# Moving a small subtraction to GpSimd, issuing weight loads earlier and re-timing two divisions in a two-layer hybrid encoder

## The chip, the cores and the metric

The kernel runs on one core of one Trainium2 chip. The metric is the device time of one execution, in microseconds. The core has five engines that run side by side and wait for each other by semaphores: TensorE (PE in the profile), VectorE (DVE), ScalarE (ACT), GpSimd (POOL), and SyncE (SP), which here issues nearly all DMAs. Each engine takes its own instructions in the order of the program, so an instruction that waits holds up everything behind it on its engine. The same is true of the DMA issues on SP.

## The reference

The reference is a trunk of two layers over 512 grid tokens and 16 learned "meta" tokens, with a model width of 1024. Cut to what matters here:

```python
def hybrid_layer(x, ...):
    h = rms_norm(x, norm_g)
    proj = einsum('bld,de->ble', h, w_in)            # 5376 columns
    qa, ka, va, za, qb, kb, vb, zb, ga, gb = split_cols(proj)
    qa, ka = rope(rms_norm(qa)), rope(rms_norm(ka))  # 8 query heads, 2 key/value heads
    oa = gqa_attention(qa, ka, va) * silu(za)        # every query sees all 528 keys
    ob = neighbourhood_attention(qb, kb, vb, rpb) * silu(zb)
    ya, yb = oa @ w_o_attn, ob @ w_o_na
    mixed = sigmoid(ga) * ya + sigmoid(gb) * yb
    return x + mixed @ w_out
```

The last step is a final RMS norm over the 512 grid tokens. The "global branch" is `gqa_attention`; the "meta keys" are the 16 meta tokens among its 528 keys.

## The kernel before

**Precision by parts.** Every float32 operand of a large product is split in two: a high part, which is a cast to the format `fp32r`, and a low part, which is the difference. A product is then three matmuls: high by high (L325), low by high (L326), high by low (L327). For a weight, ScalarE casts the high part (`whi`, L240) and GpSimd subtracts for the low part (`wlo`, L241).

**Weights in halves.** A weight chunk of 128 output columns comes as two halves of 128x512 numbers, 256 KB each. `order` is the list of all 210 halves in the sequence of their use. `weights()` (L231) is called for half `n`: it issues the loads (`raw`, L235) up to a certain place in the list and the casts and subtractions up to place `n + 2`. There are four buffers each for `raw`, `whi` and `wlo`, so a load must wait until the subtraction four halves earlier has read its buffer, and a cast until TensorE is done with the half four places earlier.

**A planner by half tiles.** TensorE works through the projections (function `product`), and after each half tile (12 or 24 matmuls with weights from memory) `tick()` lets two side plans take a step. One side plan, `side_gqa`, carries the global branch, the other, `side_na`, the neighbourhood branch. Each unit of a side plan (two 128-query tiles of one head of the global branch, or one head of the neighbourhood branch) is a list of steps, and the tables `GQA_AT` and `NA_AT` (L37 to L40) give the half tile after the unit's start at which each step is written. A list scheduler then orders each engine's instructions by priority and readiness; parts marked as high priority go first. When the projections run out, `side_na.finish()` and `side_gqa.finish()` write all remaining steps at once.

**One unit of the global branch.** `scores` computes the products of queries and keys and the exponentials. `turn` transposes 32x32 blocks on VectorE (L867) and writes the result to DRAM (`turn`, L870). `back` (L872) reads it again, transposed in full, by four DMAs (L877), and the 16+16 meta columns by a fifth into the tile `pm` (L880). `split_part` (L885) makes the high and low parts `pth` and `ptl` of the probabilities with `split` (L193 on ScalarE, L194 on VectorE). `split_ends` (L891) does the same for the meta keys: two casts on ScalarE (L896) and two subtractions on VectorE (L898) into a single padded tile `ga`, 32 partitions by 128 elements each, since a unit has two query tiles. `sums` (L901) then accumulates nine matmuls (L905): eight on `pth` and `ptl`, the ninth and last on `ga`. The two units of meta queries have one cast and one subtraction of 32x64 each.

**Inverse sums.** The softmax is not divided at once. `divided_later` (L801) has three steps for a pair of heads: `turned` takes the reciprocals of the row sums, transposes them and writes them to DRAM by four small DMAs (L811); `spread` reads them back on 64 partitions each by two DMAs (L817); `multiplied` multiplies the branch's SiLU gate by them on GpSimd (L822: `za` for the global branch, `zb` for the neighbourhood branch). The gate then multiplies the branch's output on VectorE (L777). The table entry `"divide"` gives the half tiles of the three steps.

Of the kernel before, what the change touches and what calls it, by code (L numbers as in the profile page):

```python
# [11 lines left out]
F32 = mybir.dt.float32  # L12
# [21 lines left out]
DEPTH = 2  # L34


GQA_AT = ({"scores": (0, 1), "turn": (1, 2), "back": 3, "split": (5, 5), "ends": 5, "divide": (3, 4, 6), "sums": (7, 7)},  # L37
          {"scores": (0, 1), "turn": (1, 2), "back": 3, "split": (5, 5), "ends": 5, "divide": (3, 4, 6), "sums": (7, 7)})
NA_AT = ({"stages": (0, 2, 5, 5, 5, 7), "values": (3, 4), "divide": (3, 4, 6)},
         {"stages": (0, 2, 4, 5, 5, 7), "values": (3, 4), "divide": (3, 4, 6)})  # L40

NORM_AT = ({"tokens": (0, 1, 3), "squares": (1, 1, 2, 3, 2), "heads": (2, 3, 5, 7, 6), "values": (1, 4)},
           {"tokens": (1, 3, 5), "squares": (2, 2, 2, 3, 2), "heads": (2, 3, 5, 7, 6), "values": (1, 4)})
# [52 lines left out]
def trunk_kernel(ctx: ExitStack, tc: tile.TileContext, xT, w, gn, gf, bias, rope, out):  # L96
    nc = tc.nc
# [15 lines left out]
    def slot(tag, name, dt=F32):  # L113
        n = NKEY if tag in ("KB", "KR", "K", "E") else NTOK
        t = slots.tile([P, n], dt, tag=tag, bufs=BUFS[tag], name=name)
        return t[:, :NTOK] if tag == "E" else t
# [8 lines left out]
    def bank(pool, name, tag):  # L125
        return pool.tile([P, 512], F32, tag=tag, name=name)
# [44 lines left out]
    def pad_tile(kind):  # L171
        padded[kind].rotate(1)
        return padded[kind][0]
# [17 lines left out]
    def split(hi, lo, src):  # L191
        with tc.high_priority():
            split_at["hi"] = nc.scalar.copy(hi, src)  # L193
            split_at["any"] = nc.vector.tensor_sub(lo, src, hi.bitcast(F32))  # L194
# [12 lines left out]
    order = []  # L207
    for l in range(DEPTH):
# [4 lines left out]
        if l == 0:  # L213

            order = order[6:]
# [6 lines left out]
    ready, loaded = [], []  # L222
# [7 lines left out]

    def weights(l, c, half, ahead=3):  # L231
        n = place[l, c, half] + ahead
        for l_, c_, i in order[len(loaded):n + 1]:
            raw = slots.tile([P, 4 * P], F32, tag="raw", bufs=BUFS["raw"], name=f"raw{l_}_{c_}_{i}")
            nc.sync.dma_start(raw, w[l_, c_][:, 4 * P * i:4 * P * (i + 1)])  # L235
            loaded.append(raw)
        for l_, c_, i in order[len(ready):n]:
            name, raw = f"{l_}_{c_}_{i}", loaded[len(ready)]
            hi, lo = (slots.tile([P, 4 * P], F32R, tag=tag, bufs=BUFS[tag], name=tag + name) for tag in ("whi", "wlo"))
            cast = nc.scalar.copy(hi, raw)  # L240
            sub = nc.gpsimd.tensor_sub(lo, raw, hi.bitcast(F32))  # L241
            split_at["weights"] = cast.ins, sub.ins
            ready.append((hi, lo))
        return ready[place[l, c, half]]
# [175 lines left out]
    def next_weights():  # L420
        weights(0, QA + 3, 0, 1)
        done[:] = split_at["weights"]
# [11 lines left out]
    first, ends = {}, ((0, HALF), (HALF, NTOK))  # L434
# [19 lines left out]
    for l in range(DEPTH):  # L454
# [136 lines left out]
        qs, turn = [], None  # L591
        for j in range(4):
# [188 lines left out]
        def rows2(v):  # L781
            return v.rearrange("p s d -> p (s d)")
# [64 lines left out]
        def global_unit(kv, parts, n, name, done):  # L847

            width = n * len(parts)
            per = min(4, 512 // width)  # L850

            first_token = (0, NMETA)
            c = {"t": []}

            def scores(i):
                q, qs, scale, total = parts[i]
                if i == 0:
                    c["both"] = slots.tile([P, 2 * NTOK], F32, tag="M", bufs=BUFS["M"], name=f"P{name}")
                    c["p"] = [c["both"][:, NTOK * t:NTOK * (t + 1)] for t in range(len(parts))]
                softmax(c["p"][i], q, qs, kv, NMETA - first_token[i], n, scale, total, f"{name}_{i}")  # L860

            def turn(i):

                a, b = (0, NREAL) if i == 0 and len(parts) > 1 else (NREAL * i, NREAL * i + NREAL + 32)
                if len(parts) == 1:
                    nc.gpsimd.memset(c["both"][:n, NTOK:b], 0.0)
                nc.vector.transpose(c["both"][:n, a:b], c["both"][:n, a:b])  # L867
                if i == len(parts) - 1:
                    c["there"] = dpool.tile([P, 2 * (NREAL + 32)], F32, tag="turned", bufs=3, name=f"turn{name}")
                    nc.sync.dma_start(c["there"][:n, :b], c["both"][:n, :b])  # L870

            def back():  # L872

                w, there = width * 4, c["there"][:n].rearrange("(b j) (t f) -> j t b f", j=32, t=2)
                for q in range(4):
                    r = slice(32 * q, 32 * q + 32)
                    nc.sync.dma_start(c["both"][r, :w].rearrange("j (t b x) -> j t b x", t=len(parts), x=P),  # L877
                                      there[:, :len(parts), :, P * q:P * q + P])
                c["meta"] = tiny.tile([32, P], F32, tag="meta", name=f"pm{name}")
                nc.sync.dma_start(c["meta"][:, :n].rearrange("j (b i) -> j b i", i=32),  # L880
                                  c["there"][:n].rearrange("(b j) f -> j b f", j=32)[:, :, NREAL:NREAL + 32])

            def split_part(kt):
                v = c["both"][:, :width * 4].rearrange("p (x k i) -> p x k i", k=4, i=32)[:, :, kt:kt + per]
                th, tl = slot("G", f"pth{name}_{kt}", F32R), slot("G", f"ptl{name}_{kt}", F32R)  # L885
                split(*(t[:, :width * per].rearrange("p (k x i) -> p x k i", k=per, i=32) for t in (th, tl)), v)
                for i in range(per):
                    for v in (th, tl):
                        c["t"].append((VA2[:, kt + i, kv], v[:, width * i:width * (i + 1)]))

            def split_ends():  # L891

                tm, m = pad_tile("ga"), c["meta"][:, :n]
                with tc.high_priority():
                    for t in range(len(parts)):
                        nc.scalar.copy(tm[32 * t:32 * t + 32, n * t:n * (t + 1)], m)  # L896
                    for t in range(len(parts)):
                        nc.vector.tensor_sub(tm[64 + 32 * t:96 + 32 * t, n * t:n * (t + 1)], m, tm[:32, :n].bitcast(F32))  # L898
                c["t"].append((VA2[:, 4, kv], tm[:, :width]))

            def sums(first, last):  # L901
                if first == 0:
                    c["av"] = bank(ps_a, f"av{name}", "avg")[:, :width]
                for i in range(first, last):
                    nc.tensor.matmul(c["av"], rows2(c["t"][i][0]), c["t"][i][1], start=i == 0, stop=i == 8)  # L905
                if last == 9:
                    done(c["av"])

            steps = [(at, lambda i=i: scores(i)) for i, at in zip(range(len(parts)), GQA_AT[l]["scores"])]
            for i, at in zip(range(len(parts)), GQA_AT[l]["turn"][-len(parts):]):  # L910
                steps.append((at, lambda i=i: turn(i)))
            steps.append((GQA_AT[l]["back"], back))
            n_t = 4 // per
            for i, (at, then) in enumerate(zip(GQA_AT[l]["split"][:n_t], GQA_AT[l]["sums"][-n_t:])):
                steps.append((at, lambda kt=per * i: split_part(kt)))
                f = 2 * per * (i + 1)
                steps.append((then, lambda a=2 * per * i, b=f + (f == 8): sums(a, b)))
            steps.append((GQA_AT[l]["ends"], split_ends))
            return sorted(steps, key=lambda x: x[0])

# [25 lines left out]
        def start_unit(hd, i):  # L946
# [156 lines left out]
        for j in range(4):  # L1103
            kvq[j] = {"k": slot("KR", f"kb{l}_{j}")}
            kb = kvq[j]["k"]
            for ps, a, b in project(KB + j, True):
# [5 lines left out]
                else:  # L1112
                    i, e = NREAL - HD - a, NREAL - a
# [105 lines left out]
    sums = tiny.tile([P, 50], F32, tag="mh", bufs=1, name="sums")  # L1219
# [95 lines left out]
```

## Time and profile before

| what | value |
|---|---|
| median of 3 runs | 855.81 us (853.97 to 855.95) |
| the profiled execution | 855.46 us |
| its span, first to last instruction | 853.1 us |
| PE busy | 825.1 us, 97% of the span |
| DVE / ACT / POOL busy | 552.0 / 473.7 / 382.6 us |
| mean granted TensorE clock | 0.992 |

A group's line gives the source line, the engine, the operation, the tiles out<-in, the shapes and the count, then the busy time in us and the mean duration in ns, then the idle time of that engine just before these instructions and what ended it. A row of the timeline gives the start and the duration in us, and in brackets the idle time before it. A row of the waits reads "engine line waited for releaser: us in total, times, longest us". Matmuls overlap in TensorE's pipeline, so the duration of one (some 0.28 us) is longer than the distance between two starts (some 0.12 us at 264 columns, 0.23 us at 512). SPq is SyncE's queue of DMA issues. Landmarks: layer 0's last global unit ends near 345 us, layer 0 itself near 445 us, and layer 1's last global unit near 765 us.

### The profile page before, as it was taken

How to read it: one execution, taken by the hardware profiler on the slowest of the kernel's cores; microseconds unless marked ns; L12 is line 12 of the kernel's file. 1: busy time of each engine (PE TensorE's matmuls, PEld its weight loads, DVE VectorE, ACT ScalarE, POOL GpSimd, SP SyncE). 2: the span in 40 equal slices, each digit the busy share in tenths (PEclk: the TensorE clock that was granted, in tenths of full speed). 3: DMA queues.
4: the chain of work that ended last, by engine and by line, in shares of the span. 5: the costliest groups of instructions: out<-in, count | busy, mean ns of one | idle time of the engine just before them, and what ended most of it. 6: DMA issues, size and time to landing. Idle time of an engine off the chain costs nothing.

```text
span 853.1 us, 16107 instructions
## 1 busy us (share of the span) xinstructions
PE 825.1 (97%) x5662; PEld 762.1 (89%) x5662; DVE 552.0 (65%) x1218; ACT 473.7 (56%) x1137; POOL 382.6 (45%) x296
## 2 busy tenths in 40 slices
PE   9999899989999999899999999999999999999997
PEld 9999899989999999899998989898987778878786
DVE  7976658777776675436447657777777657555633
ACT  8654677566764555333435456576757645543422
POOL 1663343343343333545765554443534433445851
PEclk9999999999999999999999999999999999999999
DMA  7277464566544564334555575657476655544502
GB/s 275 90 194 215 122 183 122 172 205 169 169 139 137 164 184 145 112 100 144 147 143 130 142 212 161 170 165 238 124 206 172 193 163 169 169 151 145 176 13 99
DMA packets 113249, 135.00 MB, mean 158 GB/s; under 512 B 31888, under 2 KB 66192, under 8 KB 113168
## 3 DMA queue, kind: packets, MB, share of 16 engines
q1 hardware_dynamic: 112448, 132.90, 53.0%
q8 instruction: 45, 0.74, 0.4%
q10 hardware_dynamic: 720, 1.06, 0.3%
q14 instruction: 36, 0.29, 0.1%
HBM read 98.50 MB, written 21.84 MB: 141 GB/s over the span
## 4 chain that ended last, share of the span: by engine, by line
PE 78%; DVE 8%; ACT 6%; issue 4%; DMA 2%; SPq 1%; POOL 1%; POOLq 0%; ACTq 0%; DVEq 0%
PE pp L327 16%; PE pp L325 16%; PE pp L326 16%; PE av L905 4%; PE y L327 3%; PE y L326 3%; PE y L325 3%; PE avb L1052 2%; DVE ptl L194 2%; PE pf L1234 2%; PE pf L1236 2%; PE pf L1235 2%; PE S L556 2%; PE S L557 1%; DVE ga L898 1%
## 5 line engine op out<-in xcount | busy, mean ns | idle before, releaser
L241 POOL TENSOR_TENSOR wlo<-raw,whi 128x512 fp32r<-128x512 f32 x210 | 289.2, 1386 | 404.7 <-ACT whi L240 325.0
L325 PE MATMUL pp<-hh,whi 128*128 128x264 f32 (+3 forms) x1040 | 326.6, 314 | 2.7 <-DVE mg L1131 1.5
L327 PE MATMUL pp<-hh,wlo 128*128 128x264 f32 (+3 forms) x1040 | 326.2, 314 | 1.3 <-POOL wlo L241 1.2
L326 PE MATMUL pp<-hl,whi 128*128 128x264 f32 (+3 forms) x1040 | 324.3, 312 | 0.0
L327 PEld LDWEIGHTS pp<-hh,wlo 128*128 128x128 f32 x1040 | 196.8, 189 | 12.9 <-POOL wlo L241 2.1
L325 PEld LDWEIGHTS pp<-hh,whi 128*128 128x128 f32 x1040 | 196.5, 189 | 12.4 <-DVE mg L1131 1.7
L326 PEld LDWEIGHTS pp<-hl,whi 128*128 128x128 f32 x1040 | 197.0, 189 | 9.5
L240 ACT CAST whi<-raw 128x512 fp32r<-128x512 f32 x210 | 127.6, 618 | 109.1 <-PE pp L326 41.1
L867 DVE STREAM_TRANSPOSE P<-P 128x512 f32<-128x512 f32 x64 | 46.4, 727 | 36.4 <-ACT P L841 35.7
L194 DVE TENSOR_TENSOR ptl<-P,pth 128x512 fp32r<-128x512 f32 x64 | 53.8, 841 | 5.4 <-ACT pth L193 4.7
L837 DVE CUSTOM_DVE_ANT_1 P<-S,r 128x528 f32<-128x528 f32 x64 | 44.9, 701 | 16.0 <-PE S L557 15.1
L1131 DVE TENSOR_TENSOR mg<-pp,rbc 128x264 f32<-128x264 f32 (+1 forms) x48 | 24.8, 517 | 39.0 <-PE pp L327 38.5
L841 ACT ACTIVATE P<-P,st 128x528 f32<-128x528 f32 x64 | 47.2, 737 | 1.9
L1132 ACT ACTIVATE mg<-mg 128x264 f32<-128x264 f32 (+1 forms) x48 | 23.7, 494 | 35.0 <-DVE mg L1131 34.8
L992 ACT ACTIVATE bias<-bias,stb 128x208 f32<-128x208 f32 (+1 forms) x64 | 31.0, 486 | 20.0 <-DVE stb L990 19.9
L193 ACT CAST pth<-P 128x512 fp32r<-128x512 f32 x64 | 39.3, 614 | 0.1
L840 ACT ACTIVATE st<-st 128x1 f32<-128x1 f32 x64 | 13.0, 203 | 45.4 <-DVE st L837 44.6
L905 PE MATMUL av<-ptl,VA 128*128 128x256 f32 x128 | 34.1, 294 | 3.3 <-DVE ptl L194 3.1
L326 PE MATMUL pp<-mx,whi 128*128 128x264 f32 x128 | 36.6, 286 | 0.0
L327 PE MATMUL pp<-mx,wlo 128*128 128x264 f32 x128 | 36.4, 284 | 0.0
L325 PE MATMUL pp<-mx,whi 128*128 128x264 f32 x128 | 36.3, 284 | 0.0
L905 PE MATMUL av<-pth,VA 128*128 128x256 f32 x128 | 34.8, 295 | 0.0
(534 smaller groups left out, 1731.6 us busy)
## 6 DMA issues: line engine op xcount, KB each, us to landing
raw<-in_w_dram SPq DMA_DIRECT2D x210, 256.0 KB
turn<-P SPq DMA_DIRECT2D x32, 528.0 KB
P<-turn SPq DMA_DIRECT2D x128, 128.0 KB
bias<-in_bias_dram SPq DMA_DIRECT2D x16, 480.0 KB
KB<-KB SPq DMA_DIRECT2D x24, 272.0 KB
rawl<-in_w_dram SPq DMA_DIRECT2D x16, 256.0 KB
x<-in_xT_dram SPq DMA_DIRECT2D x8, 264.0 KB
xr<-in_xT_dram SPq DMA_DIRECT2D x8, 264.0 KB
```

What stands on the lines that cost most here:

```text
L193: split_at["hi"] = nc.scalar.copy(hi, src)
L194: split_at["any"] = nc.vector.tensor_sub(lo, src, hi.bitcast(F32))
L240: cast = nc.scalar.copy(hi, raw)
L241: sub = nc.gpsimd.tensor_sub(lo, raw, hi.bitcast(F32))
L325: nc.tensor.matmul(ps, wh, rh[:, a:b], start=i == 0, stop=False)
L326: nc.tensor.matmul(ps, wh, rl[:, a:b], start=False, stop=False)
L327: nc.tensor.matmul(ps, wl, rh[:, a:b], start=False, stop=i == n - 1)
L837: newest["max"] = nc.vector.tensor_tensor_reduce(p[:n].rearrange("p (i k) -> p i k", i=2), S[:n, :, :HALF], scale[:n].unsqueeze(2).to_broa ...
L841: nc.scalar.activation(p[:n], p[:n], AF.Exp, bias=st[:n, 1:2], scale=1.0, accum_out=st[:n, 2:3] if total is None else total)
L867: nc.vector.transpose(c["both"][:n, a:b], c["both"][:n, a:b])
L905: nc.tensor.matmul(c["av"], rows2(c["t"][i][0]), c["t"][i][1], start=i == 0, stop=i == 8)
L992: nc.scalar.activation(pb[b], pb[b], AF.Exp, bias=st[:, b:b + 1], scale=-1.0, accum_out=total[:, b:b + 1])
```

## The change

The change has three parts. First, the subtraction of the meta keys' low parts (L898) goes from VectorE to GpSimd, 66 instructions in all. Second, `weights()` issues loads two half tiles further ahead; the casts and subtractions stay where they were in the program, and so does the number of buffers. Third, the global branch's inverse sums are taken and spread one half tile earlier (steps 2 and 3 in place of 3 and 4), and the neighbourhood branch's gate is multiplied one half tile later (step 7 in place of 6).

```diff
-GQA_AT = ({"scores": (0, 1), "turn": (1, 2), "back": 3, "split": (5, 5), "ends": 5, "divide": (3, 4, 6), "sums": (7, 7)},
+GQA_AT = ({"scores": (0, 1), "turn": (1, 2), "back": 3, "split": (5, 5), "ends": 5, "divide": (2, 3, 6), "sums": (7, 7)},
           # (the second layer's row alike)
-NA_AT = ({"stages": (0, 2, 5, 5, 5, 7), "values": (3, 4), "divide": (3, 4, 6)},
-         {"stages": (0, 2, 4, 5, 5, 7), "values": (3, 4), "divide": (3, 4, 6)})
+NA_AT = ({"stages": (0, 2, 5, 5, 5, 7), "values": (3, 4), "divide": (3, 4, 7)},
+         {"stages": (0, 2, 4, 5, 5, 7), "values": (3, 4), "divide": (3, 4, 7)})
...
     def weights(l, c, half, ahead=3):
         n = place[l, c, half] + ahead
-        for l_, c_, i in order[len(loaded):n + 1]:
+        for l_, c_, i in order[len(loaded):n + 3]:
             raw = slots.tile([P, 4 * P], F32, tag="raw", bufs=BUFS["raw"], name=f"raw{l_}_{c_}_{i}")
             nc.sync.dma_start(raw, w[l_, c_][:, 4 * P * i:4 * P * (i + 1)])
...
                     for t in range(len(parts)):
-                        nc.vector.tensor_sub(tm[64 + 32 * t:96 + 32 * t, n * t:n * (t + 1)], m, tm[:32, :n].bitcast(F32))
+                        nc.gpsimd.tensor_sub(tm[64 + 32 * t:96 + 32 * t, n * t:n * (t + 1)], m, tm[:32, :n].bitcast(F32))
```

Because a scheduler sets the order, three places show what the change moves. In the names, the digits after a tile's name are layer- or head-wise numbers and a running number, which differs between the two programs.

**VectorE in layer 0, head 2, second pair of query tiles.** `ptl` is a low part of that unit, `ga` its meta keys' low parts, `mm` a small split of the neighbourhood branch whose source bank TensorE needs back. Before:

```order
L1121 SCALAR_TENSOR_TENSOR qb_3_2780<-pp_13_264_2850,rbc_413 128x264
L194 TENSOR_TENSOR ptl_2_1_2_2833<-P_2_1_2527,pth_2_1_2_2832 128x8x2x32
L194 TENSOR_TENSOR tal_4_2882<-ta_4_2876,tah_4_2881 128x512
L898 TENSOR_TENSOR ga_120<-pm_2_1_2731,ga_120 32x128 x2
L1019 CAST mm_124<-tm_4_2885 32x16
L1020 TENSOR_TENSOR mm_124<-tm_4_2885,mm_124 32x16
```

Now:

```order
L1121 SCALAR_TENSOR_TENSOR qb_3_2784<-pp_13_264_2854,rbc_417 128x264
L1019 CAST mm_124<-tm_4_2889 32x16
L194 TENSOR_TENSOR ptl_2_1_0_2833<-P_2_1_2531,pth_2_1_0_2832 128x8x2x32
L194 TENSOR_TENSOR tal_4_2886<-ta_4_2880,tah_4_2885 128x512
L194 TENSOR_TENSOR ptl_2_1_2_2837<-P_2_1_2531,pth_2_1_2_2836 128x8x2x32
L1020 TENSOR_TENSOR mm_124<-tm_4_2889,mm_124 32x16
```

The two `ga` instructions are gone from between `tal` and `mm`; the first `ptl` of the unit now stands behind `qb`, where it stood ahead of it.

**GpSimd at the end of layer 0's global branch.** `wlo` are weights' low parts in the order of their use, `za_3` is the last gate times its inverse sums. Before:

```order
L241 TENSOR_TENSOR wlo_29_0_5001<-raw_29_0_4906,whi_29_0_5000 128x512
L241 TENSOR_TENSOR wlo_29_1_5007<-raw_29_1_4998,whi_29_1_5006 128x512
L241 TENSOR_TENSOR wlo_42_0_5100<-raw_42_0_5004,whi_42_0_5099 128x512
L241 TENSOR_TENSOR wlo_30_0_5106<-raw_30_0_5097,whi_30_0_5105 128x512
L822 TENSOR_TENSOR za_3_3207<-za_3_3207,sumsa_3_4994 128x512
```

Now:

```order
L241 TENSOR_TENSOR wlo_29_0_5005<-raw_29_0_4818,whi_29_0_5004 128x512
L898 TENSOR_TENSOR ga_120<-pm_7_0_4785,ga_120 32x128 x2
L241 TENSOR_TENSOR wlo_29_1_5011<-raw_29_1_4912,whi_29_1_5010 128x512
L241 TENSOR_TENSOR wlo_42_0_5104<-raw_42_0_4918,whi_42_0_5103 128x512
L898 TENSOR_TENSOR ga_120<-pm_7_1_4969,ga_120 32x128 x2
L822 TENSOR_TENSOR za_3_3219<-za_3_3219,sumsa_3_4971 128x512
L241 TENSOR_TENSOR wlo_30_0_5110<-raw_30_0_5002,whi_30_0_5109 128x512
```

The `ga` pairs of the last two units stand among the weights' low parts, and `za_3` stands ahead of `wlo_30_0`.

**SyncE's queue in layer 1, head 3.** `raw` are weight loads, `turn` and `P` the way of the probabilities through DRAM, `KB` and `thereb` transfers of the neighbourhood branch. Before:

```order
L235 DMA raw_21_1_8490<-in_w_dram 128x512
L235 DMA raw_25_0_8496<-in_w_dram 128x512
L870 DMA turn_3_0_8535<-P_3_0_8410 128x1056
L535 DMA KB_31_8551<-KB_30_8550 64x1088 x2
L877 DMA P_3_0_8410<-turn_3_0_8535 32x8x128
L811 DMA thereb_2_8569<-invb_2_8570 8x32
L535 DMA KB_30_8550<-KB_30_8550 64x1088
L811 DMA thereb_2_8569<-invb_2_8570 8x32 x3
L877 DMA P_3_0_8410<-turn_3_0_8535 32x8x128 x3
L880 DMA pm_3_0_8595<-turn_3_0_8535 32x4x32
L235 DMA raw_25_1_8602<-in_w_dram 128x512
L235 DMA raw_9_0_8608<-in_w_dram 128x512
```

Now:

```order
L235 DMA raw_25_1_8494<-in_w_dram 128x512
L235 DMA raw_9_0_8500<-in_w_dram 128x512
L870 DMA turn_3_0_8539<-P_3_0_8414 128x1056
L535 DMA KB_31_8555<-KB_30_8554 64x1088 x2
L811 DMA thereb_2_8573<-invb_2_8574 8x32 x4
L535 DMA KB_30_8554<-KB_30_8554 64x1088
L877 DMA P_3_0_8414<-turn_3_0_8539 32x8x128 x4
L880 DMA pm_3_0_8599<-turn_3_0_8539 32x4x32
L235 DMA raw_9_1_8606<-in_w_dram 128x512
L235 DMA raw_34_0_8612<-in_w_dram 128x512
```

The two loads `raw_25_1` and `raw_9_0` stand 13 issues earlier, ahead of `turn_3_0`. Of all 210 loads, 78 stand between 1 and 19 issues earlier among the other transfers and 5 stand later, and the order of those others hardly changes. On TensorE the order of all but 164 of 5654 instructions is the same.

More of the change, by code (lines that the diff above doesn't have):

```diff
@@ L34 @@
 DEPTH = 2
-GQA_AT = ({"scores": (0, 1), "turn": (1, 2), "back": 3, "split": (5, 5), "ends": 5, "divide": (3, 4, 6), "sums": (7, 7)},
-          {"scores": (0, 1), "turn": (1, 2), "back": 3, "split": (5, 5), "ends": 5, "divide": (3, 4, 6), "sums": (7, 7)})
-NA_AT = ({"stages": (0, 2, 5, 5, 5, 7), "values": (3, 4), "divide": (3, 4, 6)},
-         {"stages": (0, 2, 4, 5, 5, 7), "values": (3, 4), "divide": (3, 4, 6)})
+GQA_AT = ({"scores": (0, 1), "turn": (1, 2), "back": 3, "split": (5, 5), "ends": 5, "divide": (2, 3, 6), "sums": (7, 7)},
+          {"scores": (0, 1), "turn": (1, 2), "back": 3, "split": (5, 5), "ends": 5, "divide": (2, 3, 6), "sums": (7, 7)})
+NA_AT = ({"stages": (0, 2, 5, 5, 5, 7), "values": (3, 4), "divide": (3, 4, 7)},
+         {"stages": (0, 2, 4, 5, 5, 7), "values": (3, 4), "divide": (3, 4, 7)})
 NORM_AT = ({"tokens": (0, 1, 3), "squares": (1, 1, 2, 3, 2), "heads": (2, 3, 5, 7, 6), "values": (1, 4)},
```

## Prediction

> I predict 846.5 us, about 1.1% faster. The page first, for what bounds the kernel:
>
> ```profile
> PE 825.1 (97%) x5662; PEld 762.1 (89%) x5662; DVE 552.0 (65%) x1218; ACT 473.7 (56%) x1137; POOL 382.6 (45%) x296
> PE 78%; DVE 8%; ACT 6%; issue 4%; DMA 2%; SPq 1%; POOL 1%; POOLq 0%; ACTq 0%; DVEq 0%
> ```
>
> **TensorE bounds it**, and the chain of waits agrees: 78% of it is matmuls. Nothing in the change takes a matmul away, so what can be won is TensorE's idle time, 853.1 - 825.1 = 28 us, of which the start and the end (output scaling and store) are out of reach, and what an idle stretch does to the clock. So I read next who makes TensorE wait, then the granted clock by windows.
>
> ```profile
> PE tb L129 <- DVE mm L1020: 3.3, 2, 3.0
> PE av L905 <- DVE ptl L194: 3.1, 5, 1.0
> PE y L325 <- DVE mg L1131: 2.5, 1, 2.5
> PE tc L129 <- DVE mm L1020: 2.0, 1, 2.0
> PE pp L327 <- POOL wlo L241: 1.2, 2, 0.7
> PE pp L325 <- ACT whi L240: 1.1, 1, 1.1
> PE av L905 <- DVE ga L898: 1.0, 1, 1.0
> ...
> 98.00:102.00 4.00, 3.51 (x20) 3.54 (x21) 2.53 (x8) 1.44 (x4) 0.00 (x0) 0.68 0.61 169
> 102.00:106.00 4.00, 4.00 (x33) 4.00 (x32) 2.19 (x12) 1.55 (x7) 0.00 (x0) 0.89 0.45 136
> 190.00:194.00 4.00, 3.04 (x18) 3.04 (x19) 2.80 (x10) 1.08 (x3) 0.27 (x1) 0.70 0.74 210
> 194.00:198.00 4.00, 4.00 (x30) 4.00 (x31) 2.22 (x13) 3.47 (x13) 0.24 (x1) 0.87 0.67 145
> 348.00:352.00 4.00, 4.00 (x23) 4.00 (x22) 1.11 (x3) 1.03 (x3) 1.28 (x1) 0.58 0.27 75
> 230.00:234.00 4.00, 2.73 (x25) 2.59 (x24) 3.13 (x14) 2.59 (x8) 1.66 (x2) 1.00 0.84 254
> ```
>
> The first seven lines name three waits of 2 to 3 us and a scatter of waits near 1 us. The windows (length; busy time and count of PE, PEld, DVE, ACT, POOL; granted clock; DMA share; GB/s) show that each of the three long waits, at 98, 191 and 347 us, is followed by a lowered clock, while the window with a wait of 1.3 us (at 231 us) keeps 1.00. The loss behind a long wait is 4 x 0.32 + 4 x 0.11 = 1.7 us at 98 us, 4 x 0.30 + 4 x 0.13 = 1.7 us at 191 us, and 4 x 0.42 = 1.7 us at 348 us. **A long wait thus costs its length and 1.7 us more**, and shortening it to 1.5 us saves those 1.7 us too.
>
> **Part 1, the subtraction on GpSimd.**
>
> ```profile
> L898 DVE TENSOR_TENSOR ga<-pm,ga x64: 282/284/1362, 81.7 to 759.4; 32x128 fp32r<-32x128 f32 x64
> 94.26 1.78 DVE L194 TENSOR_TENSOR ptl<-P,pth 128x512 fp32r<-128x512 f32 x1
> 96.05 1.55 DVE L898 TENSOR_TENSOR ga<-pm,ga 32x128 fp32r<-32x128 f32 x2
> 188.00 2.42 DVE L898 TENSOR_TENSOR ga<-pm,ga 32x128 fp32r<-32x128 f32 x2
> 190.45 0.16 DVE L1019 CAST mm<-tm 32x16 fp32r<-32x16 f32 x1
> 187.73 2.54 POOL L241 TENSOR_TENSOR wlo<-raw,whi 128x512 fp32r<-128x512 f32 x2 [5.26 <-ACT whi L240]
> ```
>
> The subtraction takes 0.28 us at the least and up to 1.36 us (min/median/max in ns). The slow ones run beside a GpSimd subtraction: the pair at 188.00 to 190.42 lies on the two `wlo` at 187.73 to 190.27. VectorE loses 64 instructions, in its group's line 32.0 us, most of them where VectorE has slack. They count where TensorE waits for what stands behind them, in three kinds of place.
>
> (a) At 96 us: `mm` and with it TensorE come 1.55 us sooner; the wait falls from 3.0 to 1.5 us, so the clock's 1.7 us go too: 3.2 us. (b) At 188 us: without the 2.42 us the wait of 2.0 us would be gone. The order puts a `ptl` (0.69 us) between `tal` and `mm` instead, so I keep 0.5 us of wait: 1.5 + 1.7 = 3.2 us. (c) Waits near 1 us with `ga` in front:
>
> ```profile
> 260.64 1.27 DVE L898 TENSOR_TENSOR ga<-pm,ga 32x128 fp32r<-32x128 f32 x1
> 261.94 0.69 DVE L194 TENSOR_TENSOR ptl<-P,pth 128x512 fp32r<-128x512 f32 x1
> 313.18 0.38 PE L905 MATMUL av<-ga,VA 128*128 128x256 f32 x1 [0.96 <-DVE ga L898]
> 542.61 1.28 DVE L898 TENSOR_TENSOR ga<-pm,ga 32x128 fp32r<-32x128 f32 x1
> ```
>
> The first and the last stand ahead of a `ptl` that TensorE waits for (1.0 us at most each by the waits), the second is the wait on `ga` itself. That is 2.9 us at most; I take 1.7 us, since the third may only change its cause.
>
> The trace has no GpSimd subtraction of this shape. Nearest rows: 128x512 takes 1386 ns on average, and a 128x1 power 587 ns.
>
> ```profile
> L241 POOL TENSOR_TENSOR wlo<-raw,whi 128x512 fp32r<-128x512 f32 x210 | 289.2, 1386 | 404.7 <-ACT whi L240 325.0 <-PE ta L129 14.1 <-PE tc L129 9.6
> L204 POOL TENSOR_TENSOR sums<-sums,minus_half 128x1 f32<-128x1 f32 x4 | 2.3, 587 | 23.9 <-DVE sums L1260 19.4 <-DVE sums L1243 4.5
> L169 POOL MEMSET inv<- 128x32 f32 x1 | 0.1, 125 | 0.0
> ```
>
> So one costs between 0.13 us (a fill of 32 columns) and 1.39 us (no gain from being small); a quarter of the 1386 ns is 0.35 us, and with some 0.1 us fixed I take 0.45 us, 30 us for all 66 on an engine that is 45% busy and stands 325 us waiting for casts. The write goes to other partitions than the reads, which no GpSimd row shows; the upper end covers that. The Trainium skill, "GPSIMD Engine Reference", section 3, speaks against this step: two-input elementwise work is about half as fast there as on VectorE, some 2.6 cycles per element. By that figure an estimate is 128 x 2.6 / 1.2 = 277 ns plus dispatch, near the 0.45 us; the sum stays.
>
> What stands behind `ga` on GpSimd are weights' low parts, and ahead of it too, so `ga` can come late where VectorE had it in time:
>
> ```profile
> 725.53 3.79 POOL L241 TENSOR_TENSOR wlo<-raw,whi 128x512 fp32r<-128x512 f32 x3 [2.95 <-ACT whi L240]
> 724.17 0.36 PE L905 MATMUL av<-ga,VA 128*128 128x256 f32 x1
> 177.35 3.79 POOL L241 TENSOR_TENSOR wlo<-raw,whi 128x512 fp32r<-128x512 f32 x3 [5.80 <-ACT whi L240]
> 175.94 0.36 PE L905 MATMUL av<-ga,VA 128*128 128x256 f32 x1
> ```
>
> In the new order `ga` stands behind the first of the three `wlo` in the upper pair and behind the first in the lower. If those kept their times, `ga` would end near 726.8 + 0.9 = 727.7 us for a matmul that ran at 724.17, and near 178.6 + 0.9 = 179.5 us, with 177.35 + 1.27 = 178.6, for one at 175.94: 3.5 us late each. They won't keep them, as these are places where the load was late (part 2). I charge 3.0 us for the whole part (some ten of the 34 sums by 0.3 us), between a gain of ten times 0.28 = 3 us, if GpSimd is free and `ga` no longer queues behind the last `ptl`, and a loss of ten times 1.39 = 14 us.
>
> **Part 2, loads two half tiles further ahead.** In most of the kernel a load is issued the moment its buffer is free, and can't be sooner:
>
> ```profile
> SPq L235 <- POOL wlo L241: 221.0, 113, 7.9
> SPq L870 <- DVE P L867: 60.1, 16, 6.9
> ...
> 608.66 0.33 SPq L870 DMA_DIRECT2D turn<-P  x1
> 619.92 0.42 SPq L235 DMA_DIRECT2D raw<-in_w_dram  x1
> 624.71 1.08 SPq L235 DMA_DIRECT2D raw<-in_w_dram  x2
> 628.39 1.59 POOL L241 TENSOR_TENSOR wlo<-raw,whi 128x512 fp32r<-128x512 f32 x1 [1.36 <-DMA therea<-inva]
> 643.21 2.99 POOL L241 TENSOR_TENSOR wlo<-raw,whi 128x512 fp32r<-128x512 f32 x2 [8.64 <-ACT whi L240]
> ```
>
> 113 loads wait at the head of the queue for a `wlo`. Where the attention's transfers fill the queue it is the reverse: the queue waits for a transposition (60.1 us in all) and loads stand behind it. At 620 to 645 us this reaches TensorE: the waits on `wlo` and `whi`, 1.2 + 1.1 = 2.3 us, lie there. In the new queue the loads of 619 us stand ahead of `turn_3_0`, which was issued at 608.66, so they come 10 us sooner: I count all 2.3 us as won. The price is a transfer held up behind a load that waits for its buffer. In most places the load stands in front of something that itself waits; the rest I charge with 0.5 us, between 0 and 6 (one wait of the longest kind, 7.9 us, less the slack of a half tile or two).
>
> **Part 3, the divisions.**
>
> ```profile
> 343.51 1.28 POOL L822 TENSOR_TENSOR za<-za,sumsa 128x512 f32<-128x512 f32 x1
> 344.82 1.75 DVE L777 TENSOR_TENSOR oa<-oa,za 128x528 f32<-128x528 f32 x1 [2.00 <-POOL za L822]
> 347.18 0.36 PE L325 MATMUL y<-oa_0a,whi 128*128 128x264 f32 x1 [2.55 <-DVE mg L1131]
> ```
>
> At the end of layer 0's global branch GpSimd runs three `wlo`, then `za`; VectorE stands 2.00 us for it, the evacuation `mg` stands behind VectorE, and TensorE waits 2.55 us. In the new order `za_3` passes one `wlo` (1.3 us) but stands behind the last `ga` pair (0.9 us), and earlier loads let the others start sooner. Between nothing and 2.0 + 1.7 = 3.7 us, I take 2.5 us. The neighbourhood branch's multiplication, one half tile later, meets its sums already landed; `ob` (L777) follows it behind nine to eleven matmuls, a copy and an addition, over 2 us against its 1.3 us: nothing.
>
> **The sum**: 3.2 + 3.2 + 1.7 + 2.3 + 2.5 = 12.9 us won, 3.0 + 0.5 = 3.5 us lost, 9.4 us net. The profiled execution took 855.46 us (span 853.1 and 2.4 around it), 0.35 below the median: 855.46 - 9.4 = 846.1, and to the median's side 846.5 us.
>
> On the clock the Trainium skill, "TensorE: Matmul & The Clock Gate", Part 1, says that the clock halves after an idle window of about 3.4 us. The three waits here are 2.0 to 3.0 us long and the clock still fell, so the trace sets the limit lower. By the page's figure no clock would be won: an estimate of 5 us less, 851.5 us.
>
> **Rivals.**
>
> *GpSimd's queue becomes the bound* (slower). `ga` stands behind a `wlo` whose cast waits for a load or for TensorE, TensorE's ninth matmul waits for `ga`, and with TensorE stalled the next cast is late too. For it: in the trace before, the two places above would each be 3.5 us late. Against: loads come sooner just there. If ten of 34 sums lose 1.8 us each, 18 us in place of 3, the time is 855.5 - 12.9 + 18 + 0.5, near 861 us; it decides from about 1.2 us per such sum, where the 12.9 - 0.5 us are used up. Chance 0.15.
>
> *The gain is handed on.* VectorE is 65% busy, and what stood behind `ga` at 96 and 188 us may still be late, by its own contention with `wlo` (the `ptl` at 94.26 took 1.78 us in place of 0.69). Then (a) and (b) give half, the clock still falls, and 1.5 + 1.5 + 2.3 - 3.5 leaves about 2 us: 854 us. For it: the waits come from several things in a row. Against: the long pairs were themselves on the chain. Chance 0.20.
>
> *Everything lands*: no late `ga`, the full 3.7 us at 347 us and 2.9 us in (c): 855.5 - 3.2 - 3.2 - 2.9 - 2.3 - 3.7, near 840 us. Chance 0.13.
>
> *The loads do nothing* because casts and not loads were late: 2.3 us less and some late `ga`, which lies within the forecast.
>
> **The numbers.** The forecast, 843 to 850.5 us, has 0.52. The range of 8 in 10 reaches to 839.5 and to 857. A measurement here tells 0.3%, 2.6 us, from no change. Faster by more: the forecast, everything lands, and a few hundredths of the second rival, 0.69. Within: most of the second rival and the edge of the first, 0.18. Slower: 0.13.
>
> **What would show it.** Right: no clock below 0.95 near 98, 191 and 347 us; the waits of `tb` and `tc` on `mm` under 1.5 us; no wait of `pp` on `wlo` near 620 to 645 us; L898 on POOL near 0.45 us. Wrong: a total wait of `av` on `ga` over 5 us, L898 over 0.8 us, SPq waiting longer than 221 us for `wlo` with `turn` or `P` behind it and `pth` waiting for DMA, or the three dips still there.

## The result, and the profile after

The changed kernel takes 845.63 us (median of 4 runs, 844.70 to 846.45) against 854.98 us (853.97 to 855.95) of the kernel before: ratio 0.9891, 95% interval 0.9872 to 0.9910. The forecast was 846.5 us. Its profiled execution took 845.68 us, with a span of 844.0 us.

The page of the changed kernel: busy times, the chain by engine, and the group of the moved subtraction (count | busy us, mean ns | idle before).

```profile
PE 821.0 (97%) x5662; PEld 757.9 (90%) x5662; DVE 522.8 (62%) x1152; ACT 474.8 (56%) x1137; POOL 422.8 (50%) x362
...
PE 85%; DVE 6%; ACT 3%; issue 2%; DMA 2%; SPq 1%; POOL 0%; POOLq 0%; DVEq 0%; ACTq 0%
...
L898 POOL TENSOR_TENSOR ga<-pm,ga 32x128 fp32r<-32x128 f32 x64 | 40.4, 632 | 47.9 <-issue 26.8
```

The waits of TensorE in the changed kernel (us in total, times, longest):

```profile
PE av L905 <- DVE ptl L194: 3.7, 7, 0.8
PE tb L129 <- DVE tal L194: 3.5, 3, 1.5
PE y L325 <- ACT oa_3a L193: 2.4, 1, 2.4
PE y L325 <- ACT ob L193: 1.5, 1, 1.5
...
PE pp L327 <- POOL wlo L241: 0.6, 1, 0.6
```

The granted clock of the changed kernel over the two places at 98 and 191 us, and then over its end of layer 0 (window; length; busy us of PE, PEld, DVE, ACT, POOL; clock; DMA share; GB/s):

```profile
94.00:106.00 12.00, 11.85 (x99) 11.45 (x98) 7.13 (x28) 8.11 (x25) 5.74 (x5) 1.00 0.57 156
186.00:198.00 12.00, 11.70 (x98) 11.55 (x98) 7.51 (x29) 7.92 (x26) 4.76 (x5) 1.00 0.74 183
...
339.50:342.91 3.41, 1.13 (x6) 0.84 (x6) 2.01 (x4) 2.08 (x4) 3.16 (x3) 1.00 0.07 6
342.91:346.32 3.41, 3.13 (x15) 3.00 (x14) 2.68 (x4) 1.25 (x2) 3.41 (x3) 0.50 0.56 180
```

The waits on `mm` are gone, and the first two clock dips with them. The waits on `wlo` and `whi` near 620 to 645 us are gone too (the one on `wlo` that is left lies at 331 us), and no wait on `ga` is left. The third dip stands, behind a wait of 2.4 us at the end of layer 0 that now has another cause (`oa_3a`, not `mg`). And there are waits that the kernel before did not have, on `oa_3a` and on `ob`, or had shorter: 3.5 us on `tal` against 1.5 us. Whether each of the three parts gave what it was expected to give cannot be read from this trace, so the parts were taken apart.

### The profile page after: what moved, and what is told of

It reads as the page before. It is cut to its first block, busy times and chain, and to the rows that moved or that the text cites. A ratio compares the mean times of both kernels' runs of the same rounds, so it can differ in the third digit from the quotient of the medians.

```text
span 844.0 us, 16154 instructions
## 1 busy us (share of the span) xinstructions
PE 821.0 (97%) x5662; PEld 757.9 (90%) x5662; DVE 522.8 (62%) x1152; ACT 474.8 (56%) x1137; POOL 422.8 (50%) x362
## 4 chain that ended last, share of the span: by engine, by line
PE 85%; DVE 6%; ACT 3%; issue 2%; DMA 2%; SPq 1%; POOL 0%; POOLq 0%; DVEq 0%; ACTq 0%
PE pp L327 18%; PE pp L325 18%; PE pp L326 18%; PE av L905 4%; PE y L326 3%; PE y L327 3%; PE y L325 3%; DVE ptl L194 2%; PE avb L1052 2%; PE S L556 2%; PE S L557 2%; PE pf L1234 2%; PE pf L1236 2%; PE pf L1235 2%; PE tb L129 1%
## 5 line engine op out<-in xcount | busy, mean ns | idle before, releaser
L327 PEld LDWEIGHTS pp<-hh,wlo 128*128 128x128 f32 x1040 | 196.4, 189 | 11.2 <-POOL wlo L241 0.8
L898 POOL TENSOR_TENSOR ga<-pm,ga 32x128 fp32r<-32x128 f32 x64 | 40.4, 632 | 47.9 <-issue 26.8
L194 DVE TENSOR_TENSOR ptl<-P,pth 128x512 fp32r<-128x512 f32 x64 | 55.6, 881 | 12.8 <-ACT pth L193 10.3
```

Source lines behind the costliest of these rows:

```text
L327: nc.tensor.matmul(ps, wl, rh[:, a:b], start=False, stop=i == n - 1)
L898: nc.gpsimd.tensor_sub(tm[64 + 32 * t:96 + 32 * t, n * t:n * (t + 1)], m, tm[:32, :n].bitcast(F32))
```

## A run's time in two shares

The three dips of the kernel before, in windows of 3.41 us cut at the switches of the clock (same columns), then the same stretch of part 1 alone, and of part 1 with half of part 3:

```profile
96.06:99.47 3.41, 0.98 (x9) 1.01 (x10) 2.89 (x6) 0.32 (x1) 1.10 (x1) 1.00 0.42 96
99.47:102.88 3.41, 3.41 (x17) 3.41 (x17) 1.53 (x4) 1.12 (x4) 0.00 (x0) 0.50 0.72 237
188.22:191.63 3.41, 1.38 (x12) 1.20 (x12) 2.94 (x5) 0.73 (x2) 2.05 (x2) 1.00 0.85 255
191.63:195.04 3.41, 3.41 (x19) 3.38 (x18) 2.67 (x12) 1.46 (x5) 0.00 (x0) 0.50 0.53 140
345.23:348.64 3.41, 1.46 (x12) 1.49 (x13) 2.83 (x4) 1.75 (x4) 1.26 (x2) 1.00 0.41 131
348.64:352.05 3.41, 3.41 (x17) 3.41 (x17) 0.84 (x2) 0.73 (x2) 0.79 (x1) 0.50 0.28 77
```

```profile
331.35:334.76 3.41, 1.68 (x14) 1.47 (x13) 1.54 (x1) 0.05 (x1) 3.06 (x3) 1.00 0.47 154
334.76:338.17 3.41, 2.59 (x21) 2.62 (x22) 2.12 (x5) 1.90 (x4) 1.29 (x1) 1.00 0.23 77
```

```profile
333.87:337.28 3.41, 1.22 (x10) 1.25 (x11) 3.06 (x4) 1.51 (x4) 1.27 (x2) 1.00 0.42 146
337.28:340.69 3.41, 3.41 (x17) 3.41 (x17) 0.43 (x1) 0.53 (x2) 1.03 (x1) 0.50 0.27 77
```

In every trace the clock is either 1.00 or 0.50, and the distance between two switches is a multiple of 3.413 us (99.47 to 191.63 us is 27 of them, 191.63 to 348.64 us is 46). So the clock is set per window of a fixed grid, and a lowered window that is full of matmuls costs 3.41 x 0.50 = 1.7 us. The grid lies differently against the program in each execution. The same wait of 2.5 us at the end of layer 0 therefore has a dip behind it in the kernel before, none in part 1 alone, and one again in the third kernel: TensorE was busy for 1.46, 1.68 and 1.22 us of the window that decides. Over the fourteen profiles of this study, all 15 windows with less than 0.43 of TensorE's busy time (between 60 and 790 us) were followed by one at 0.50; between 0.45 and 0.58 some were and most were not; above that no dip began.

The dips are thus partly chance, and a fair comparison takes them out. The span times its mean granted clock is what the span would be at full clock; the rest of the span is the clock's share. The clock is listed to three digits, which leaves 0.4 us open in each value. The share also holds the end of each profile, where the clock is at 0.50 again but TensorE's last matmul is over: 0.4 to 1.8 us that cost nothing and differ by execution. So differences of under 1 us in the table say little.

| kernel | parts | median us | ratio to before (95%) | span at full clock, mean (range) us | clock's share, mean us |
|---|---|---|---|---|---|
| before | none | 853.8 | | 847.2 (845.3 to 848.7; 44 runs) | 5.1 |
| e1_ga | 1 | 842.24 | 0.9868 (0.9852 to 0.9884) | 837.5 (836.3 to 838.3) | 2.7 |
| e2_loads | 2 | 860.72 | 1.0084 (1.0071 to 1.0097) | 852.0 (850.0 to 853.1) | 7.3 |
| e3_div | 3 | 859.09 | 1.0058 (1.0041 to 1.0076) | 849.9 (848.8 to 850.9) | 7.1 |
| e4_loads_div | 2, 3 | 860.08 | 1.0078 (1.0058 to 1.0098) | 851.3 (850.6 to 852.1) | 7.4 |
| e5_ga_div | 1, 3 | 847.21 | 0.9922 (0.9901 to 0.9944) | 839.9 (838.9 to 840.6) | 5.6 |
| e6_ga_loads | 1, 2 | 850.36 | 0.9955 (0.9940 to 0.9969) | 843.6 (843.0 to 844.3) | 5.0 |
| after | 1, 2, 3 | 845.63 | 0.9891 (0.9872 to 0.9910) | 840.1 (839.6 to 840.6) | 3.8 |

The runs of the kernel before spread from 850.61 to 857.55 us, while their spans at full clock lie within 3.4 us: about half of that spread is the clock.

## Experiments: the three parts alone and in pairs

**Part 1 alone.**

```diff
-  nc.vector.tensor_sub(tm[64 + 32 * t:96 + 32 * t, ...
+  nc.gpsimd.tensor_sub(tm[64 + 32 * t:96 + 32 * t, ...
```

> Part 1 alone: the subtraction of the meta keys' low parts on GpSimd, loads and divisions as before. Theory A (the parts add up, and part 1 is the largest): the places at 98 and 191 us are repaired by it alone, so the clock in the windows 98 to 106 and 190 to 198 us is 1.00, the time falls by 8.1 - 3.0 = 5 us to about 850 us, ratio 0.994. Theory B (part 1 only pays with part 2, since without earlier loads `ga` stands behind `wlo` whose loads are late): the two clock dips are gone too, but TensorE waits for `ga` on GpSimd, over 5 us in all, most of it near 177 and 725 us, and the time falls by less than 2 us or rises. Theory C (earlier loads carry the gain): within 1 us of the kernel before, and at least one of the two dips is still there.

Measured: 842.24 us, 3.4 us **less than the whole change**. Of theory A the mechanism held and the size did not: twice the gain, 11.4 us. Theories B and C fell. VectorE at the first place, in part 1 alone (start, duration, instruction):

```profile
93.14 0.67 DVE L194 TENSOR_TENSOR ptl<-P,pth 128x512 fp32r<-128x512 f32 x1
94.26 0.43 DVE L1121 SCALAR_TENSOR_TENSOR qb<-pp,rbc 128x264 f32<-128x264 f32 x1 [0.45 <-PE pp L327]
94.81 0.16 DVE L1019 CAST mm<-tm 32x16 fp32r<-32x16 f32 x1
```

The `ptl` that took 1.78 us in the kernel before, beside a GpSimd subtraction, stands 1.1 us earlier here and takes 0.67 us, and `mm` comes 3.2 us earlier, not 1.55 us. The waits on `mm` at 98 and 191 us (3.2 and 2.2 us by the distance of matmul starts) are gone altogether.

**Part 2 alone, part 3 alone, and both without part 1.**

```diff
-        for l_, c_, i in order[len(loaded):n + 1]:
+        for l_, c_, i in order[len(loaded):n + 3]:
```

> Part 2 alone: loads two half tiles further ahead. Theory A: the waits of TensorE on `wlo` and `whi` at 620 to 645 us go (2.3 us), the dips at 98 and 191 us stay, the time falls by 1.8 us to about 853 us, ratio 0.998. Theory B: the same or less. Theory C: at least one of the dips at 98 and 191 us is gone, and the time falls by 5 us or more, ratio 0.994 or lower.

```diff
-GQA_AT = (... "divide": (3, 4, 6) ...    NA_AT = (... "divide": (3, 4, 6) ...
+GQA_AT = (... "divide": (2, 3, 6) ...    NA_AT = (... "divide": (3, 4, 7) ...
```

> Part 3 alone: the divisions at other half tiles. As predicted: TensorE's wait at 347 us (2.7 us) and the clock behind it repaired, 2.5 us less, about 852.5 us, ratio 0.997. By the trace of the changed kernel, where a wait of 2.4 us and a clock of 0.71 are still found at 341 to 348 us: nothing, within 1 us of the kernel before.

Both of the last two edits, without the first:

> Parts 2 and 3 without part 1 (the changed kernel with the subtraction back on VectorE). Theory A: 5 us slower than the changed kernel, about 851 us, ratio 0.995, with the dips at 98 and 191 us as before. Theory B (part 1 pays only with part 2): more than 5 us slower than the changed kernel, near 853 us, ratio 0.998. Theory C: within 2 us of the changed kernel, 846 to 848 us, ratio 0.991.

Measured: 860.72, 859.09 and 860.08 us. Every theory had these parts between a gain and nothing; **each of them makes the kernel slower**, by 0.84%, 0.58% and 0.78%. A part of that is the clock: their profiles keep the dip at 98 us and have 2 to 4 dips each.

**Part 1 with one of the others.** The edits are those above.

> Parts 1 and 3 without the earlier loads. Measured so far: part 1 alone 842.2 us, all three 845.6 us, so parts 2 and 3 together cost 3.4 us beside part 1. Theory D (the loads carry that cost, because a load that waits for its buffer holds up the reading of the inverse sums behind it): 841 to 843.5 us, ratio 0.986. Theory E (the divisions carry it, because they put eight small transfers ahead of loads): 846 us or more, ratio 0.991, with TensorE waiting over 1.5 us each for `wlo` near 340 and 565 us and over 2 us for `na` near 590 us, as with part 3 alone.

> Parts 1 and 2 without the divisions. Theory D: part 2 costs here what it cost alone, 842.2 + 7 = 849 us, ratio 0.995, with the wait of the output projection at the end of layer 0 near 4 us and the reading of `sumsa` issued some 5 us late there; part 3 then wins 3 us back by standing earlier. Theory E: 842 us or less, ratio 0.986, since the divisions are gone.

Measured: 847.21 and 850.36 us. Theory E's number came out for the first, theory D's for the second: each part costs beside part 1. With the eight kernels of the table, at full clock: part 1 wins 9.7 us alone and 8.4 to 11.2 us beside the others. Part 2 costs 4.8 us alone and 6.1 us beside part 1, but only 0.2 us beside parts 1 and 3. Part 3 costs 2.7 us alone and 2.4 us beside part 1, but wins 3.5 us beside parts 1 and 2. Parts 2 and 3 repair each other's damage, and what is left of it in the whole change is 840.1 - 837.5 = 2.6 us. The single profiles say much the same: by span less 1.7 us for each lowered window ahead of the end, part 1 wins 9.5 us, parts 2 and 3 cost 6.1 and 3.5 us beside it, and the two together 3.8 us.

## Experiments: why earlier loads cost

SyncE's queue at the end of layer 0, in the kernel before and then with part 2 alone (`sumsa` is the reading of the inverse sums):

```profile
330.23 1.30 SPq L235 DMA_DIRECT2D raw<-in_w_dram  x3
331.70 1.12 SPq L817 DMA_DIRECT2D sumsa<-therea  x2
```

```profile
331.37 5.46 SPq L235 DMA_DIRECT2D raw<-in_w_dram  x3
337.05 1.12 SPq L817 DMA_DIRECT2D sumsa<-therea  x2
```

The three loads wait for buffers and hold `sumsa` up by 5.4 us. That was theory D's reason, and in part 2 alone it is there, though `za`, which needs `sumsa`, ran only at 350.24 us there, behind three `wlo`. And beside part 1 `sumsa` was issued at 329.62 us, in good time, and TensorE waited 4.2 us all the same. What differs is TensorE's own order. Part 1 alone, from the last sum of the global branch on, and then parts 1 and 2 (in each, the first row is the last unit's ninth matmul):

```profile
330.06 0.29 PE L905 MATMUL av<-ga,VA 128*128 128x256 f32 x1
330.19 0.28 PE L327 MATMUL pp<-hh,wlo 128*128 128x264 f32 x1
...
332.75 0.28 PE L327 MATMUL pp<-hh,wlo 128*128 128x264 f32 x1
335.58 0.37 PE L325 MATMUL y<-oa_0a,whi 128*128 128x264 f32 x1 [2.55 <-DVE mg L1131]
```

```profile
338.67 0.28 PE L905 MATMUL av<-ga,VA 128*128 128x256 f32 x1
343.19 0.81 PE L325 MATMUL y<-oa_3a,whi 128*128 128x264 f32 x2 [4.24 <-ACT oa_3a L193]
```

In part 1 alone 22 projection matmuls stand behind the last sum and cover 2.7 us of the chain copy, `oa`, `za`, cast; the output projection comes after them. With earlier loads the scheduler has written those matmuls, and 18 of the output projection's 24, **ahead** of the last sum. Nothing is left to cover the chain. GpSimd in parts 1 and 2, and then in the changed kernel:

```profile
336.32 4.19 POOL L241 TENSOR_TENSOR wlo<-raw,whi 128x512 fp32r<-128x512 f32 x3 [2.81 <-issue]
340.47 1.26 POOL L822 TENSOR_TENSOR za<-za,sumsa 128x512 f32<-128x512 f32 x1
```

```profile
338.47 1.27 POOL L822 TENSOR_TENSOR za<-za,sumsa 128x512 f32<-128x512 f32 x1
339.99 6.33 POOL L241 TENSOR_TENSOR wlo<-raw,whi 128x512 fp32r<-128x512 f32 x4 [0.25 <-ACT whi L240]
```

As in part 1 alone, `za` stands behind three `wlo` in parts 1 and 2, and VectorE stands 1.95 us for it. The changed kernel has 18 matmuls of the output projection ahead of the last sum too, but its `za` runs ahead of the `wlo`, and TensorE waits 2.4 us and not 4.2 us. That is what part 3 repairs here.

To test what the order on TensorE costs, the loads near that place were put back:

```diff
-        for l_, c_, i in order[len(loaded):n + 3]:
+        for l_, c_, i in order[len(loaded):n + (1 if 68 <= n <= 84 else 3)]:
```

> Parts 1 and 2, but with the loads as before for places 68 to 84 of the list (the end of layer 0's global branch). Parts 1 and 2 whole took 850.4 us, part 1 alone 842.2 us. Theory D (most of what part 2 costs is the reading of the last inverse sums, held up behind three loads that wait for buffers): TensorE's wait at the end of layer 0 falls from 4.2 us to 2.5 us with fewer halved windows of the clock behind it, about 846 us, ratio 0.991. Rival (the cost is spread over the late `ptl` of the whole kernel): within 1 us of parts 1 and 2 whole, 849.5 to 851 us.

Measured: 845.56 us (0.9894, 0.9877 to 0.9912), full clock 841.2 us against 843.6. The order of TensorE there is again that of part 1 alone, and the wait is 2.6 us, on `mg`. Theory D's number is met, by a mechanism it did not have. This place is thus worth 2.4 us at full clock, and 4.8 us in the medians with the dips behind the long wait. The other 841.2 - 837.5 = 3.7 us that part 2 costs beside part 1 are small waits, as the rival had it: 3.3 us on `tal` and 4.5 us on `ptl` in this trace, where part 1 alone has 0.8 and 2.3 us.

## Experiments: why earlier divisions cost

ScalarE at the end of layer 0 in part 1 alone, and then in parts 1 and 3:

```profile
328.01 1.14 ACT L240 CAST whi<-raw 128x512 fp32r<-128x512 f32 x2
330.39 0.36 ACT L769 COPY cmb<-av 64x256 f32<-64x256 f32 x1 [1.24 <-PE av L905]
```

```profile
330.32 0.36 ACT L769 COPY cmb<-av 64x256 f32<-64x256 f32 x1 [2.09 <-PE av L905]
330.71 1.14 ACT L240 CAST whi<-raw 128x512 fp32r<-128x512 f32 x2
```

TensorE's waits in parts 1 and 3:

```profile
PE pp L327 <- POOL wlo L241: 4.5, 4, 1.4
PE pp L325 <- ACT whi L240: 2.8, 3, 1.1
PE avb L1052 <- DVE na L798: 2.4, 1, 2.4
```

The wait on `mg` at the end of layer 0 is gone, as the prediction's part 3 wanted it, but the reading of the inverse sums now stands ahead of three weight loads in SyncE's queue. Two casts that stood ahead of the copy `cmb` stand behind it, and TensorE waits for `whi` and `wlo` in the place of `mg`, there and near 221, 559 and 636 us; the wait on `na`, at 586 us, is longer too (1.0 us in part 1 alone). To see which half of part 3 it is:

```diff
-NA_AT = (... "divide": (3, 4, 6) ...
+NA_AT = (... "divide": (3, 4, 7) ...
```

> Part 1 and only the neighbourhood branch's half of part 3 (its gate multiplied at step 7 in place of 6). Parts 1 and 3 whole took 847.2 us, part 1 alone 842.2 us. As the prediction had it, this half does nothing: within 1 us of part 1 alone, ratio 0.986, and the 5 us that part 3 costs are those of the global branch's inverse sums, whose transfers stand ahead of weight loads. Rival: the late gate costs, 845 us or more, with the wait of 2.5 us on `na` near 586 us found here too.

Measured: 842.97 us (0.9871, 0.9844 to 0.9898), full clock 838.1 us against 837.5 of part 1 alone. The neighbourhood half does nothing; the cost is, by difference, the global half's, which was not run alone.

## Experiments: what the subtraction costs on GpSimd

```diff
+                        for _ in range(2):
                             nc.gpsimd.tensor_sub(tm[64 + 32 * t:96 + 32 * t, ...
```

> Part 1 alone, with the subtraction on GpSimd issued twice: the second one writes the same numbers again, so the output is the reference's. It adds some 66 x 0.5 = 30 us of work to GpSimd. Theory F (GpSimd has room, and a late `ga` costs nothing): within 1.5 us of part 1 alone, 842 to 844 us. Rival G (the queue on GpSimd decides, the prediction's first rival): ten or more of the 34 sums come 0.5 to 0.9 us later, 5 to 9 us more, 847 to 851 us, with a wait of `av` on `ga` of over 4 us.

The second kernel has no subtraction there at all:

> Part 1 alone, with the subtraction left out altogether: the low parts of the meta keys' probabilities are not computed, and their rows of `ga` keep what they held. It asks what the subtraction costs on GpSimd. Theory F (it costs nothing there): within 1.5 us of part 1 alone, 841 to 843.5 us. The prediction's charge: 3 us faster than part 1 alone, near 839 us. Rival G: 5 us or more faster, 837 us or less.

Measured: 852.66 us twice (0.9975, 0.9962 to 0.9989) and 841.09 us without (0.9843, 0.9826 to 0.9861), around 842.24 us once. So the first copy costs 1.15 us, which is within the scatter of these runs, and the second 10.4 us. At full clock it is 0.9 and 6.7 us. Theory F's half on leaving it out holds, and its half on doubling fell. The waits of TensorE with the doubled subtraction (line numbers are one higher in this kernel):

```profile
PE pp L327 <- POOL wlo L241: 4.9, 5, 2.0
PE y L325 <- DVE mg L1132: 3.1, 1, 3.1
PE pp L325 <- DVE mg L1132: 2.4, 1, 2.4
PE av L906 <- POOL ga L899: 2.0, 4, 0.7
```

Rival G named the queue rightly, but not the size (847 to 851 us) and not the victim: TensorE waits only 2.0 us in all for `ga` itself. What comes late is what stands behind it on GpSimd, the weights' low parts and the gate's product that `mg` waits for (VectorE stands 3.8 us for `za`, 2.0 us with one copy). GpSimd is 51% busy with one copy and 54% with two, so the average says nothing of this.

## Experiments: a faster version

Two waits of part 1 alone, at 336 and 665 us, stand behind a product on GpSimd. VectorE there, in part 1 alone, and then with the last pair's products on VectorE:

```profile
333.22 1.75 DVE L777 TENSOR_TENSOR oa<-oa,za 128x528 f32<-128x528 f32 x1 [2.00 <-POOL za L822]
...
663.18 0.69 DVE L777 TENSOR_TENSOR ob<-ob,zb 128x512 f32<-128x512 f32 x1 [3.19 <-POOL zb L822]
```

```profile
329.27 1.76 DVE L822 TENSOR_TENSOR za<-za,sumsa 128x512 f32<-128x512 f32 x1
331.06 0.43 DVE L773 TENSOR_TENSOR oa<-av,cmb 64x256 f32<-64x256 f32 x1
331.53 1.22 DVE L777 TENSOR_TENSOR oa<-oa,za 128x528 f32<-128x528 f32 x1
```

```diff
-                nc.gpsimd.tensor_mul(g[:, :NREAL], ...
+                (nc.vector if name.endswith("_3") else nc.gpsimd).tensor_mul(g[:, :NREAL], ...
```

> Part 1 alone, and the last pair's gates (`za_3`, `zb_3` of both layers) multiplied by their inverse sums on VectorE in place of GpSimd, four instructions. Theory H (the waits of 2.7 us at 336 us and of 1.7 us at 665 us come from the place of that multiplication in GpSimd's queue, behind weights' low parts, and not from inverse sums that come late): VectorE stood 2.0 and 3.2 us for these two products, so both waits of TensorE fall below 1 us, some 3 us are won, and 1.7 us more where a clock dip goes: about 838.5 us, ratio 0.982. Rival (the inverse sums themselves are late, as the prediction's part 3 had it): within 1 us of part 1 alone, 842 us, and VectorE waits at the same places for a transfer.

Measured: 837.31 us (0.9799, 0.9781 to 0.9816), full clock 833.8 us against 837.5. Theory H holds. The inverse sums had long landed; the product runs at 329.27 us, in time that VectorE had spare, and TensorE's waits at the two places fall to 0.5 us and below. So what held the chain up was a place in GpSimd's queue, and not a late transfer.

On top of that, earlier loads only where loads had been late ("the kernel before in this list" is the one just shown):

```diff
-        for l_, c_, i in order[len(loaded):n + 1]:
+        for l_, c_, i in order[len(loaded):n + (3 if 158 <= n <= 166 else 1)]:
```

> As the kernel before in this list, and the loads of 9 of the 210 half tiles (places 158 to 166 of the list, layer 1 near 600 to 630 us) two half tiles further ahead, the others as before. Theory A's remaining half (earlier loads pay only where a load stood late behind transfers of the attention): the waits on `wlo` and `whi` at 613 to 631 us go, 2.8 us by part 1's trace; about 836 us, ratio 0.979. Rival (what they win there, later transfers of probabilities give back as waits on `ptl`): within 1 us of the kernel without these loads.

Measured: 836.75 us (0.9789, 0.9772 to 0.9806), full clock 833.9 us, the same as without. TensorE's waits in it:

```profile
PE av L905 <- DVE ptl L194: 3.0, 4, 1.0
...
PE pp L325 <- ACT whi L240: 1.1, 1, 1.1
...
PE pp L327 <- POOL wlo L241: 0.9, 1, 0.9
```

By the distance of matmul starts, the waits at 611 to 629 us went, 2.8 us. A wait on `ptl` of 1.3 us at 646 us and waits on `whi` and `wlo` of 2.4 us at 743 us came: the rival's number, and in part its reason. Still, both versions are faster than the kernel before and the changed kernel, by some 2.0% and 1.0%.

## Why the prediction was right, and where it was not

The time was right, 9.4 us forecast and 9.35 us measured, but **by errors of both signs**. Part 1 was to give 8.1 - 3.0 = 5.1 us and gives 11.4 us (9.7 at full clock); parts 2 and 3 were to give 2.3 - 0.5 + 2.5 = 4.3 us and cost 3.4 us (2.6). That leaves 8.0 us; the other 1.3 us lie between the medians of the kernel before in the two sessions (854.98 and 853.64 us). That the total agreed this closely was luck: the sum had two wrong signs in it and one term at half its size.

- *(a) and (b), the long pairs.* Right in mechanism and undersized. The 1.5 and 0.5 us of wait that were to remain did not. At 96 us only `ga` itself was counted, not that the `ptl` ahead of it would come out from beside the `wlo` (1.78 to 0.67 us).
- *(c), the scattered waits.* Undersized: 1.7 us were taken. By the distance of matmul starts, the waits at 231, 247, 262, 313, 545 and 765 us fall by 0.6, 0.2, 0.8, 1.1, 0.2 and 0.3 us in part 1 alone, 3.2 us. With the 3.2 and 2.2 us above that is 8.6 us of the 9.7 us; where the rest lies was not found.
- *The price on GpSimd.* 0.45 us was the least (451 ns), and in part 1 alone about the median (460 ns); the mean is 0.63 us in the changed kernel, so 40.4 us and not 30. It mattered little: the charge of 3.0 us was 1.15 us. The places at 177 and 725 us did not come late. The prediction put that down to the earlier loads; part 1 alone has none, and TensorE waits for `ga` nowhere in it. The upper end was in reach, though: another 37 us of such work cost 10.4 us.
- *"A long wait thus costs its length and 1.7 us more."* The 1.7 us are right as the price of a dip, and wrong as a rule for a wait: the same 2.5 us at the end of layer 0 has a dip behind it in three profiles (the kernel before, part 1 without the subtraction, part 1 with half of part 3) and none in two others (part 1 alone, and the kernel with the loads put back). It also fails the other way: in the first faster version a dip begins at 629 us, behind waits of 1.1 and 0.5 us that fell into one window.
- *Part 2, "I count all 2.3 us as won".* Those waits did go, in the changed kernel and in the last version. The step that failed is "the rest I charge with 0.5 us, between 0 and 6": it measured 4.8 us alone and 6.1 us beside part 1. And it looked for the price only in SyncE's queue. One term beside part 1, 2.4 of the 6.1 us by putting the loads back at one place, came with TensorE's order: work that had covered the end of a stage was written ahead of it. The larger term, 3.7 us in small waits on `ptl` and `tal`, has no cause shown.
- *Part 3, 2.5 us.* Failed as a gain of its own. The place was read rightly: `za` stood behind `wlo` on GpSimd, and it stands ahead of them in the changed kernel. But alone the step traded a wait on `mg` for waits on weights; beside part 2 it wins 3.5 us, of which 1.8 us of wait are seen at the end of layer 0. The last pair's products moved to VectorE won 3.7 us without that price. That the neighbourhood half does nothing was right.
- *The rivals.* "GpSimd's queue becomes the bound" did not occur with one subtraction, and did with two. "The gain is handed on" fell, and "the loads do nothing" was too kind to them.
- *The marks.* No dip near 98 and 191 us, no wait on `mm`, none on `wlo` near 620 us: met. No dip near 347 us, and L898 near 0.45 us: not met. Of the signs of being wrong one came up: SyncE's queue waited 255.7 us for `wlo`, against 221.0 us, and `pth` waited once, 1.3 us, for a DMA, which it did nowhere before. This is part 2's doing: the queue waited 251.1 us with it alone and 220.0 us with part 1 alone.

Open: which of part 2's changes of order makes `tal` and `ptl` late in the rest of the kernel, 3.7 us.

## What to carry to other kernels

Take a change of several parts apart even when the forecast of the whole comes out: here one part won 11 us and the other two gave back 3. Under a scheduler, work that is made available earlier moves the bounding engine's own instructions too, so look at what will still cover the end of each stage. Before an operation is made earlier, see whether its consumer waits for its inputs or for its place in a queue; four products on another engine won more than all re-timing.

## What the runs showed of the hardware

TensorE's clock is set per window of 3.413 us on a grid that does not follow the program, and it halved behind each of the 15 windows in which TensorE was busy for 1.46 us or less; the three of the kernel before, with waits of 2 to 3 us, were still busy for 0.98, 1.38 and 1.46 us. The Trainium skill, "TensorE: Matmul & The Clock Gate", Part 1, describes a free-running window of 3413 ns, and the traces agree with both; it gives a whole idle window as the condition, and here less was enough. About half of the scatter of a kernel's runs (850.6 to 857.6 us for the kernel before) goes with it: at full clock the same runs lie within 3.4 us.
